# Third mixer with two heads in one product of scores, bias as a product with ones, sink as a column, and other places for the activations' tiles

## The chip, the cores and the metric

One NeuronCore of a Trainium2 chip runs the whole network in one launch. The metric is device time in microseconds (us). Matrix products run on TensorE (PE), elementwise work on VectorE (DVE), ScalarE (ACT) and GpSimd (POOL); transfers are issued from SyncE (SP).

## What is computed

Four layers on 256 tokens of width 1024, in fp32. Each is a half feed-forward block, a mixer and another half feed-forward block, with norms before and after. Layers 0 and 3 have the dilated mixer, layer 1 the differential one, layer 2 the sliding-window mixer with bias and sinks:

```python
for i in range(4):
    x = x + 0.5 * rms_norm(swiglu(rms_norm(x, ...), gate, up, down), ...)
    x = x + rms_norm(mixer_i(rms_norm(x, ...)), ...)
    x = x + 0.5 * rms_norm(swiglu(rms_norm(x, ...), gate, up, down), ...)

def swa_sink_attention(h, w_in, b_in, w_out, sinks):      # layer 2
    proj = h @ w_in + b_in        # 16 query heads of 64, 2 key heads, 2 value heads
    s = q @ k.T / 8 - slope * dist              # masked to the last 128 tokens
    m = max(max(s), sink)
    p = exp(s - m); denom = sum(p) + exp(sink - m)
    return ((p / denom) @ v) @ w_out
```

## The kernel before

A product in fp32 is three products on parts (`mm3`): each operand is split into a high part `h` (a cast to fp32r) and the remainder `l`, and `hi*h`, `hi*l`, `lo*h` are added up in PSUM. Weights stream from HBM into `raw` (three buffers) and are split into `hi` (ScalarE, line 142) and `lo` (VectorE, or GpSimd in the mixers, line 143), four buffers each. Activations are split the same way into `xTh`, `xTl` (normed input, transposed), `hTh`, `hTl` (feed-forward hidden) and `oTh`, `oTl` (a mixer's output).

In `mm3` the first operand is stationary (loaded into the array) and the second moves through it. In a row of the profile, `out<-moving,stationary`. In the feed-forward block, `gu` are the products of 512 columns for gate and up (stationary `xT`, moving weights), `acc` those for the way down (stationary `hT`). In a mixer, `lead` and `v` have `xT` stationary and weights moving, `qk` has weights stationary and `xT` moving; `sc` are scores, `tp` transposes, `o` weighted values; `acc` on `oT` closes the mixer.

A partition of SBUF is filled pool by pool: constants, then `raw`, `hi`, `lo` of 8192 bytes each, then `x`, gains, work tiles and `xTh`, `xTl`, then small tiles, then the block's own tiles, which begin with `hTh`, `hTl` or `oTh`, `oTl`.

The third mixer (`kind == 2`) works in 16 units, one head each, over both blocks of 128 queries. `biased` adds the bias on VectorE while the projection is read from PSUM. `stack_q` and `stack_k` place high and low parts in the two halves of the partitions, so that a head's score takes two products of 128 partitions (line 525) per block of queries. Then come minimum (line 756), exponential (759), the sink's exponential (762), its addition (784), the reciprocal, the normalisation (791), four transposes (800), the split of `p` (817, 818) and the products with `v`. The loop over `slot` works a unit's steps in different slots, with projections (`rest`) and then the closing product in between. A list scheduler sets the order on each engine; queues run in that order. The bias comes from two small transfers: `cbt` at the program's start, `cbv` (line 438) at this mixer's start.

Of the kernel before, what the change touches and what calls it, by code (L numbers as in the profile page):

```python
# [29 lines left out]
NACT = 0  # L30
# [16 lines left out]
def tile_network(  # L47
# [16 lines left out]
    c_bias_t: bass.AP,  # L64
    c_bias_v: bass.AP,
# [119 lines left out]
    cbt = const.tile([P, 9], F32, name="cbt")  # L185
    sink = const.tile([P, 16], F32, name="sink")
    nsink = const.tile([P, 16], F32, name="nsink")
# [34 lines left out]
    def norm_elem(t, s, parts=1):  # L222
# [9 lines left out]
        hn_of[t] = hn  # L232
# [35 lines left out]
    def norm_tr_(t):  # L268
        hn = hn_of.pop(t)
        if t == 0:  # L270
            new_xT()
# [67 lines left out]
    def ffn(layer, which):  # L339
        s = 3 * layer + 2 * which  # L340
        with ExitStack() as c:
            fp = c.enter_context(tc.tile_pool(name="ffn", bufs=2, reuse_waits="tile"))
            hTh = fp.tile([P, KF, SEQ], F32R, name="hTh", bufs=1)
            hTl = fp.tile([P, KF, SEQ], F32R, name="hTl", bufs=1)
# [75 lines left out]
    def mixer(layer):  # L420
# [3 lines left out]
        with ExitStack() as c:  # L424
            mp = c.enter_context(tc.tile_pool(name="mix", bufs=2, reuse_waits="tile"))
            oTh = mp.tile([P, KD, SEQ], F32R, name="oTh", bufs=1)
            oTl = mp.tile([P, KD, SEQ], F32R, name="oTl", bufs=1)
# [60 lines left out]
            def biased(src, bias, sc):  # L488
                tmp = mp.tile([P, SEQ], F32, tag="cq", name="cq", bufs=2)
                dve.tensor_scalar(out=tmp, in0=src, scalar1=bias, scalar2=sc, op0=ALU.add, op1=ALU.mult)  # L490
                return tmp

# [10 lines left out]
            def stack_q(z, e, src, sc):  # L503

                own, other = halves(e)
                if sc is None:
                    act.copy(out=z[own], in_=src[own])
                    dve.tensor_tensor(out=z[other], in0=src[own], in1=z[own].bitcast(F32), op=ALU.subtract)
                    return
# [67 lines left out]
            def token_major(i, k, k0, o, t, step):  # L577
# [581 lines left out]
```

## Time and profile before

| | us |
|---|---|
| median of 3 runs | 2340.42 (2339.28 to 2341.62) |
| the profiled execution | 2340.16 |
| its span, first to last instruction | 2338.4 |
| first mixer | 201 to 486 of the span |
| third mixer | 1370.7 to 1479.8 of the span |

Times in rows are from the span's start. PE ends are modelled, so spacing is read from the starts of successive products. "Idle before" says how long the engine stood before that group, and the arrow what ended it. A row of windows has the engines in the order PE, PEld (loads of the stationary operand), DVE, ACT, POOL, then the granted TensorE clock, the DMA share and GB/s.

### The profile page before, as it was taken

What the parts mean: (1) busy time and instruction counts of PE and PEld (TensorE: products, weight loads), DVE (VectorE), ACT (ScalarE), POOL (GpSimd) and SP (SyncE); (2) the same over time, 40 slices, a digit from 0 to 9 for tenths busy, and PEclk for the clock granted to TensorE, in tenths of its full rate; (3) what the DMA queues carried; (4) which work ended last, traced back from release to release, by engine and by line L of the source; (5) the groups of instructions that cost most, each with busy time, mean ns of one, the idle gap of its engine ahead of it and who ended that gap; (6) DMA issues with size and microseconds to landing.
All of it is one profiled execution on the core that took longest, in us unless ns stands there. A gap on an engine that the chain in (4) does not pass through costs nothing.

```text
span 2338.4 us, 32427 instructions
## 1 busy us (share of the span) xinstructions
PE 2295.4 (98%) x12906; PEld 2012.5 (86%) x12906; DVE 1267.0 (54%) x1858; ACT 1201.3 (51%) x2117; POOL 628.3 (27%) x618
## 2 busy tenths in 40 slices
PE   8999999999999999999999988999999999999998
PEld 6889999988888889788888877788888899998887
DVE  6555444565565555665465459654555544446553
ACT  5445655654444447654354447544444466665442
POOL 0005877620020028610020042100200287774000
PEclk9999999999999999999999999999999999999999
DMA  7544444445555554265455541455454444443552
GB/s 285 195 177 171 163 149 150 153 182 196 181 191 190 187 179 158 77 239 188 180 198 191 188 153 67 180 180 182 186 208 181 181 174 146 143 154 136 216 180 90
DMA packets 60776, 404.71 MB, mean 173 GB/s; under 512 B 7120, under 2 KB 8144, under 8 KB 16592
## 3 DMA queue, kind: packets, MB, share of 16 engines
q1 hardware_dynamic: 60480, 402.57, 47.7%
q8 instruction: 101, 1.65, 0.3%
q14 instruction: 51, 0.42, 0.1%
q10 hardware_dynamic: 144, 0.07, 0.0%
HBM read 401.56 MB, written 1.05 MB: 172 GB/s over the span
## 4 chain that ended last, share of the span: by engine, by line
PE 90%; DVE 4%; ACT 2%; POOL 2%; DMA 1%; issue 1%; SPq 0%; POOLq 0%; DVEq 0%; ACTq 0%
PE gu L177 11%; PE gu L176 11%; PE gu L175 11%; PE acc L175 8%; PE acc L176 8%; PE acc L177 8%; PE qk L175 4%; PE qk L177 4%; PE qk L176 4%; PE v L175 2%; PE v L177 2%; PE v L176 2%; PE tp L369 2%; PE tp L800 1%; PE u L177 1%; PE u L176 1%
## 5 line engine op out<-in xcount | busy, mean ns | idle before, releaser
L142 ACT CAST hi<-raw 128x1024 fp32r<-128x1024 f32 (+2 forms) x970 | 774.6, 844 | 769.2 <-PE gu L177 322.1
L143 DVE TENSOR_TENSOR lo<-raw,hi 128x1024 fp32r<-128x1024 f32 (+1 forms) x546 | 659.5, 1246 | 553.3 <-ACT hi L142 553.3
L143 POOL TENSOR_TENSOR lo<-raw,hi 128x512 fp32r<-128x512 f32 (+1 forms) x424 | 545.5, 1318 | 204.9 <-ACT hi L142 198.2
L175 PE MATMUL gu<-hi,xTh 128*128 128x512 f32 (+1 forms) x1280 | 474.2, 370 | 0.0
L177 PE MATMUL gu<-hi,xTl 128*128 128x512 f32 (+1 forms) x1280 | 471.2, 368 | 0.0
L176 PE MATMUL gu<-lo,xTh 128*128 128x512 f32 (+1 forms) x1280 | 470.9, 368 | 0.0
L215 POOL TENSOR_SCALAR ms<-ssf 128x1 f32<-128x1 f32 x24 | 8.3, 347 | 1415.5 <-ACT junk L244 1414.4
L176 PE MATMUL acc<-lo,hTh 128*128 128x512 f32 x704 | 279.0, 396 | 0.0
L175 PE MATMUL acc<-hi,hTh 128*128 128x512 f32 x704 | 277.1, 394 | 0.0
L177 PEld LDWEIGHTS gu<-hi,xTl 128*128 128x128 f32 x1280 | 241.3, 188 | 39.8
L177 PE MATMUL acc<-hi,hTl 128*128 128x512 f32 x704 | 275.5, 391 | 0.0
L176 PEld LDWEIGHTS gu<-lo,xTh 128*128 128x128 f32 x1280 | 241.4, 189 | 39.3
L175 PEld LDWEIGHTS gu<-hi,xTh 128*128 128x128 f32 x1280 | 241.4, 189 | 39.1
L175 PE MATMUL qk<-xTh,hi 128*128 128x256 f32 x800 | 228.7, 286 | 0.0
L177 PE MATMUL qk<-xTh,lo 128*128 128x256 f32 x800 | 226.0, 282 | 0.0
L176 PE MATMUL qk<-xTl,hi 128*128 128x256 f32 x800 | 225.8, 282 | 0.0
L177 PEld LDWEIGHTS acc<-hi,hTl 128*128 128x128 f32 x704 | 132.2, 188 | 29.9
L175 PEld LDWEIGHTS acc<-hi,hTh 128*128 128x128 f32 x704 | 132.3, 188 | 29.2
L176 PEld LDWEIGHTS acc<-lo,hTh 128*128 128x128 f32 x704 | 132.4, 188 | 26.9
L176 PEld LDWEIGHTS qk<-xTl,hi 128*128 128x128 f32 x800 | 152.6, 191 | 0.1
L177 PEld LDWEIGHTS qk<-xTh,lo 128*128 128x128 f32 x800 | 152.6, 191 | 0.0
L175 PEld LDWEIGHTS qk<-xTh,hi 128*128 128x128 f32 x800 | 152.5, 191 | 0.0
(242 smaller groups left out, 3376.4 us busy)
## 6 DMA issues: line engine op xcount, KB each, us to landing
raw<-in_w_ffn_dram SPq DMA_DIRECT2D x263, 1024.0 KB, 4.8
raw<-in_w_a_qk_dram SPq DMA_DIRECT2D x48, 1024.0 KB, 4.8
raw<-in_w_a_v_dram SPq DMA_DIRECT2D x32, 768.0 KB, 4.3
raw<-in_w_a_out_dram SPq DMA_DIRECT2D x8, 1024.0 KB, 4.8
raw<-in_w_b_qk_dram SPq DMA_DIRECT2D x8, 1024.0 KB, 4.8
gain<-in_g_pre_dram SPq DMA_DIRECT2D x12, 512.0 KB, 6.3
gain<-in_g_post_dram SPq DMA_DIRECT2D x12, 512.0 KB, 8.3
raw<-in_w_b_v_dram SPq DMA_DIRECT2D x4, 1024.0 KB, 4.9
```

Source lines behind the costliest of these rows:

```text
L142: act.copy(out=hi[:, cs], in_=r[:, cs])
L143: eng.tensor_tensor(out=lo[:, cs], in0=r[:, cs], in1=hi[:, cs].bitcast(F32), op=ALU.subtract)
L175: pe.matmul(o, lhsT=a[0], rhs=b[0], start=first, stop=False)
L176: pe.matmul(o, lhsT=a[0], rhs=b[1], start=False, stop=False)
L177: pe.matmul(o, lhsT=a[1], rhs=b[0], start=False, stop=last)
L215: pool.tensor_scalar(out=ms, in0=a, scalar1=b, scalar2=EPS, op0=ALU.add, op1=ALU.add)
L369: pe.transpose(tp[:, i * P:(i + 1) * P], h[:, i * P:(i + 1) * P], ident)
L800: pe.transpose(tp[:, c0:c0 + P], sp[:, i * P:(i + 1) * P], ident)
```

## The change

The third mixer is written anew, and tiles of activations move.

- A unit is now two heads and one block of queries. Keys lie in `kc` (`kch`, `kcl`): the first key head in the first 64 partitions and 256 columns, the second in the others, zeros elsewhere. One `mm3` of 512 columns gives both heads' scores. `stack_q`, `stack_k` and `biased` go from this mixer; `q` is split whole (`store_scaled`).
- The bias comes as a row `cb`: its high part in partition 0, its low part in partition 32, zeros elsewhere. One more product with a tile of ones adds it in PSUM. `cb` is built at the mixer's start from five transfers, each cast by ScalarE and subtracted by VectorE.
- The negated sink is a 257th column of a score's row, written by GpSimd, so the exponential's sum has it.
- `xTh`, `xTl` become one tile `xT`, whose two parts begin 192 bytes later in a mixer; `hT` and `oT` become one tile each. `nsink` gets 64 bytes more, so that weights stay where they were. In the built program the first byte of each tile in a partition, divided by 256, leaves: weights 224 before and after; `xT` 224, after 224 in a feed-forward block and 160 in a mixer; `hT` and `oT` 160, after 224. In the first mixer `pw` leaves 224 and `vh` 160, before and after.

```diff
+    NX, NH = KD * SEQ, KF * SEQ
+    def two(z, o, n):
+        return [z[:, o + i * n:o + (i + 1) * n].rearrange("p (k n) -> p k n", n=SEQ) for i in range(2)]
-    def new_xT():
-        xT["h"] = actp.tile([P, KD, SEQ], F32R, tag="xTh", name="xTh")
-        xT["l"] = actp.tile([P, KD, SEQ], F32R, tag="xTl", name="xTl")
+    def new_xT(s):
+        z = actp.tile([P, 2 * NX + 64], F32R, tag="xT", name="xT")
+        xT["h"], xT["l"] = two(z, 48 if s % 3 == 1 else 0, NX)
...
+            hTh, hTl = two(fp.tile([P, 2 * NH], F32R, name="hT", bufs=1), 0, NH)
...
+            oTh, oTl = two(mp.tile([P, 2 * NX + 48], F32R, name="oT", bufs=1), 0, NX)
...
-                cbv = mp.tile([P, P], F32, name="cbv", bufs=1)
-                nc.sync.dma_start(out=cbv, in_=c_bias_v.partition_broadcast(P))
+                cb = mp.tile([P, D + 256], F32R, name="cb", bufs=1)
+                ones = mp.tile([P, SEQ], F32R, name="ones", bufs=1)
+                pool.memset(cb.bitcast(F32), 0.0)
+                pool.memset(ones.bitcast(F32), 1.0)
+                for i in (4, 0, 1, 2, 3):
+                    cs = slice(i * 256, (i + 1) * 256)
+                    cbf = mp.tile([P, 2, 260], F32, tag="sp", name="cbf", bufs=5)[:, 0, :256]
+                    nc.sync.dma_start(out=cbf[:1], in_=c_bias[:, cs])
+                    act.copy(out=cb[:1, cs], in_=cbf[:1])
+                    dve.tensor_tensor(out=cb[32:33, cs], in0=cbf[:1], in1=cb[:1, cs].bitcast(F32), op=ALU.subtract)
...
-                        tmp = biased(ov[:, f], cbt[:, b:b + 1], qsc[:, 16 + b:17 + b])
-                        qk[gr].append([stack(f"q{f}{e}", 4) for e in range(2)])
-                        for e in range(2):
-                            stack_q(qk[gr][f][e], e, tmp, None)
+                        h, l = pair(f"q{f}", [P, SEQ], 4)
+                        store_scaled(h, l, ov[:, f], qsc[:, 16 + b:17 + b])
+                        qk[gr].append((h, l))
...
+                    if last and bias is not None:
+                        pe.matmul(o, lhsT=ones[:, :P], rhs=bias, start=False, stop=True)
...
-                    tmp = biased(tp[:, :SEQ], cbt[:, 8:9], 1.0)
-                    qk["k"] = [stack(f"k{e}", 1, True) for e in range(2)]
-                    for e in range(2):
-                        stack_k(qk["k"][e], e, tmp)
+                    for i in range(2):
+                        rows = slice(64 * i, 64 * i + 64)
+                        store(kc[0][rows, i], kc[1][rows, i], tp[rows, :SEQ])
...
+                            pe.matmul(of, lhsT=cb[:, b * P:(b + 1) * P], rhs=ones, start=True, stop=False)
...
-                        scores_of(dst, q2[:, bs], k2)
+                    pool.tensor_scalar(out=sp[:, :, 256], in0=nsink.rearrange("p (e i) -> p i e", e=2)[:, hd],
+                                       scalar1=1.0, scalar2=None, op0=ALU.mult)
+                    mm3(sc, (h[:, bs], l[:, bs]), [z.rearrange("p e n -> p (e n)") for z in kc], True, True)
...
-                    act.activation(out=se, in_=nm, func=AF.Exp, bias=sink[:, hd:hd + 1], scale=1.0)
...
-                    dve.tensor_tensor(out=den, in0=den, in1=se, op=ALU.add)
```

Outside the third mixer the order on every engine stays as it was. On VectorE, ahead of that mixer's first scores, before (`vl` the values' low part, `cq` a biased projection, `k`, `q` the stacked halves; line 756 the first minimum):

```order
L481 TENSOR_TENSOR vl<-cvt,vh 128x128
L490 TENSOR_SCALAR cq<-tp,cbt 128x256
L519 TENSOR_TENSOR k_12422<-cq,k_12422 64x256
L519 TENSOR_TENSOR k_12423<-cq,k_12423 64x256
L520 COPY k_12422<-k_12422 64x512
L520 COPY k_12423<-k_12423 64x512
L490 TENSOR_SCALAR cq<-tp,cbt,qsc 128x256 x2
```

and at the same place after:

```order
L448 TENSOR_TENSOR cb<-cbf,cb 1x256 x4
L497 TENSOR_TENSOR vl<-lead,vh 128x128
L497 TENSOR_TENSOR kcl<-tp,kch 64x256 x2
L501 SCALAR_TENSOR_TENSOR q0l<-tp,qsc,q0h 128x256
L771 ISA sp,nm<-sc,dist,nsink 128x256
```

Five instructions for the keys, four on `cq` and four on `q` (the last six of them not shown) that stood before the first minimum have become two on `kcl` and one on `q0l`; those on `cb` are new. On ScalarE at the mixer's start, before (`vh`, `tok` are read from the projections, `xTh` is the second token half):

```order
L226 ACTIVATE hn,ssx<-x 128x1024
L480 CAST vh<-cvt 128x128
L615 COPY tok<-lead 128x128
L617 COPY tok<-lead 128x256 x2
L279 CAST xTh<-tp 128x4x128 x2
```

and after:

```order
L229 ACTIVATE hn,ssx<-x 128x1024
L447 CAST cb<-cbf 1x256
L496 CAST vh<-lead 128x128
L282 CAST xT<-tp 128x4x128
L624 COPY tok<-lead 128x128
L282 CAST xT<-tp 128x4x128
L447 CAST cb<-cbf 1x256 x4
```

The cast of the bias's first piece now stands where `vh` stood; `vh` waits for a bias product on TensorE, which needs that piece.

## Rows read from the trace of the kernel before

**Rows 1.** The page's first part: busy us, share of the span, instructions.

```profile
PE 2295.4 (98%) x12906; PEld 2012.5 (86%) x12906; DVE 1267.0 (54%) x1858; ACT 1201.3 (51%) x2117; POOL 628.3 (27%) x618
```

**Rows 2.** Windows of the first mixer: stretch, length, busy us and instructions by engine.

```profile
201.00:486.00 285.00, 284.57 (x2136) 279.28 (x2135) 144.43 (x312) 178.17 (x400) 200.45 (x184) 1.00 0.44 156
```

**Rows 3.** PE by time: first and last start of four unbroken runs of products.

```profile
42.50 0.40 PE L176 MATMUL gu<-lo,xTh 128*128 128x512 f32 x1
...
63.81 0.40 PE L177 MATMUL gu<-hi,xTl 128*128 128x512 f32 x1
...
145.13 0.39 PE L176 MATMUL acc<-lo,hTh 128*128 128x512 f32 x1
...
196.40 0.40 PE L175 MATMUL acc<-hi,hTh 128*128 128x512 f32 x1
...
231.14 0.28 PE L175 MATMUL qk<-xTh,hi 128*128 128x256 f32 x1
...
238.21 0.28 PE L177 MATMUL qk<-xTh,lo 128*128 128x256 f32 x1
...
261.37 0.28 PE L175 MATMUL o<-pw,vh 128*128 128x256 f32 x1
...
262.61 0.28 PE L177 MATMUL o<-pw,vl 128*128 128x256 f32 x1
```

**Rows 4.** Windows of the third mixer's middle.

```profile
1396.80:1421.90 25.10, 16.08 (x113) 14.63 (x111) 24.30 (x59) 17.93 (x50) 14.26 (x11) 0.92 0.31 119
1421.90:1440.10 18.20, 14.86 (x71) 11.29 (x71) 16.66 (x53) 14.22 (x42) 5.12 (x4) 0.92 0.26 81
1440.10:1462.90 22.80, 21.93 (x110) 17.93 (x110) 20.30 (x72) 17.00 (x52) 2.78 (x3) 0.93 0.07 29
```

**Rows 5.** Waits in that stretch: us in total, times, longest.

```profile
PE tp L800 <- DVE sp L791: 5.6, 6, 3.1
...
PE sc L525 <- DVE q L508: 4.0, 1, 4.0
```

**Rows 6.** Products of line 175: shape, count, busy us and mean ns, idle before.

```profile
L175 PE MATMUL acc<-hi,hTh 128*128 128x512 f32 x704 | 277.1, 394 | 0.0
...
L175 PE MATMUL qk<-xTh,hi 128*128 128x256 f32 x800 | 228.7, 286 | 0.0
...
L175 PE MATMUL v<-hi,xTh 128*128 128x384 f32 x224 | 77.6, 346 | 0.0
...
L175 PE MATMUL lead<-hi,xTh 128*128 128x256 f32 x192 | 55.4, 289 | 1.6 <-ACT xTh L279 0.9 <-DVE u L250 0.7
...
L175 PE MATMUL acc<-hi,oTh 128*128 128x512 f32 x128 | 54.0, 422 | 0.9 <-ACT oTh L881 0.7
...
L175 PE MATMUL v<-hi,xTh 128*128 128x256 f32 x48 | 13.8, 288 | 0.0
```

**Rows 7.** VectorE in that stretch; then one form each of VectorE and GpSimd elsewhere.

```profile
L508 DVE TENSOR_TENSOR q<-cq,q 64x256 fp32r<-64x256 f32 x16 | 9.9, 620 | 0.5
...
L784 DVE TENSOR_TENSOR den<-den,se 128x2 f32<-128x2 f32 x16 | 4.0, 251 | 0.0
L490 DVE TENSOR_SCALAR cq<-tp,cbt,qsc 128x256 f32<-128x256 f32 x6 | 3.0, 540 | 0.3 <-PE tp L627 0.2
...
L485 DVE SCALAR_TENSOR_TENSOR ql<-tp,qsc,qh 128x256 fp32r<-128x256 f32 x3 | 1.5, 485 | 6.8 <-ACT qh L484 6.7
...
L452 POOL MEMSET dg10h<- 64x256 f32 x2 | 0.6, 308 | 0.1
```

**Rows 8.** The third mixer's start by time; last, transfers with KB and us to landing.

```profile
1383.60 0.29 DVE L613 TENSOR_TENSOR cvt<-lead,cbv 128x128 f32<-128x128 f32 x1 [2.96 <-DMA cbv<-in_c_bias_v_dram]
...
1385.48 0.39 PE L175 MATMUL lead<-hi,xTh 128*128 128x256 f32 x1 [0.92 <-ACT xTh L279]
...
1379.00 0.43 SPq L193 DMA_DIRECT2D gain<-in_g_post_dram  x1
...
gain<-in_g_post_dram SPq DMA_DIRECT2D x1, 512.0 KB, 9.3
```

More of the change, by code (lines that the diff above doesn't have):

```diff
@@ L29 @@
 PIECES = 2
-NACT = 0
 RAW = 3
@@ L436, in mixer @@
             elif kind == 2:
-                cbv = mp.tile([P, P], F32, name="cbv", bufs=1)
-                nc.sync.dma_start(out=cbv, in_=c_bias_v.partition_broadcast(P))
+                cb = mp.tile([P, D + 256], F32R, name="cb", bufs=1)
[7 more added lines that the diff above has]
+                    act.copy(out=cb[:1, cs], in_=cbf[:1])
+                    dve.tensor_tensor(out=cb[32:33, cs], in0=cbf[:1], in1=cb[:1, cs].bitcast(F32),
+                                      op=ALU.subtract)
+                kc = [mp.tile([P, 2, SEQ], F32R, name=f"kc{c_}", bufs=1) for c_ in "hl"]
+                for v in kc:
+                    pool.memset(v[:64, 1].bitcast(F32), 0.0)
+                    pool.memset(v[64:, 0].bitcast(F32), 0.0)
             qk = {}
@@ L599, in head @@
                 k = KD // nv if what == "v" else KD
-                yield from token_major(ids[n], k, k * m if what == "v" else 0, o, t, step)
+                c0 = D if what == "kv" else 256 * gr
+                yield from token_major(ids[n], k, k * m if what == "v" else 0, o, t, step,
+                                       cb[:, c0:c0 + 256] if kind == 2 else None)
                 if t:
@@ L607, in head @@
                 if t == 0:
-                    tok[n] = mp.tile([P, 2, 256], F32, tag="sp", name="tok", bufs=(3, 6, 5)[kind])
+                    tok[n] = mp.tile([P, 2, 260 if kind == 2 else 256], F32, tag="sp", name="tok", bufs=(3, 6, 5)[kind])[:, :, :256]
                 if what == "kv":
@@ L611, in head @@
                         vv["v"] = pair("v", [P, 2, P], 1)
-                    vt = mp.tile([P, P], F32, tag="cvt", name="cvt")
-                    dve.tensor_tensor(out=vt, in0=o[:, P:], in1=cbv, op=ALU.add)
-                    store(vv["v"][0][:, t], vv["v"][1][:, t], vt)
+                    store(vv["v"][0][:, t], vv["v"][1][:, t], o[:, P:])
                     act.copy(out=tok[n][:, t, :P], in_=o[:, :P])
@@ L758, in scores @@
-                for _, dst, _, m, dn in parts:
-                    act.activation(out=dst, in_=dst, func=AF.Exp, scale=-1.0, bias=m, accum_out=dn)
-                if kind == 2:
-                    se = small.tile([P, 2], F32, tag="se", name="se")
-                    act.activation(out=se, in_=nm, func=AF.Exp, bias=sink[:, hd:hd + 1], scale=1.0)
-                    st[u] = (spb.rearrange("p b n -> p (b n)"), dnb, se)
+                    b = e
+                    h, l = qk[gr][f]
+                    sp = mp.tile([P, 2, 260], F32, tag="sp", name="sp", bufs=5)
@@ new lines, in scores @@
+                    parts = [(sc[:, i * 256:(i + 1) * 256], sp[:, i], dist[:, b], nm[:, i:i + 1],
+                              den[:, i:i + 1], sl_n[hd + 8 * i], nsink[:, hd + 8 * i:hd + 8 * i + 1], 257)
+                             for i in range(2)]
+                    st[u] = (sp, den, None)
+                for src, dst, d, m, _, sl, init, n in parts:
+                    dve.tensor_tensor_reduce(out=dst[:, :src.shape[-1]], in0=src, in1=d, scale=-sl, scalar=init,
+                                             op0=ALU.add, op1=ALU.min, accum_out=m)
@@ L765, in normalised @@
+                for _, dst, _, m, dn, _, _, n in parts:
+                    act.activation(out=dst[:, :n], in_=dst[:, :n], func=AF.Exp, scale=-1.0, bias=m, accum_out=dn)
             def normalised(u):
-                sp, den, se = st.pop(u)
+                sp, den, _ = st.pop(u)
                 rd = small.tile([P, 2], F32, tag="rd", name="rd")
@@ L783, in normalised @@
                 else:
-                    dve.tensor_tensor(out=den, in0=den, in1=se, op=ALU.add)
                     dve.reciprocal(out=rd, in_=den)
-                    for b in range(2):
-                        v = sp[:, b * 256:(b + 1) * 256]
-                        if b < NACT:
-                            act.activation(out=v, in_=v, func=AF.Copy, scale=rd[:, b:b + 1])
-                        else:
-                            dve.tensor_scalar(out=v, in0=v, scalar1=rd[:, b:b + 1], scalar2=None, op0=ALU.mult)
+                    for i in range(2):
+                        v = sp[:, i, :256]
+                        dve.tensor_scalar(out=v, in0=v, scalar1=rd[:, i:i + 1], scalar2=None, op0=ALU.mult)
                 st[u] = sp
```

76 lines of the change are left out of this document (29 added, 47 removed).

## The prediction

> **What bounds the kernel now.** I read the page's first part, then the engines by stage, then groups of matmuls with their counts, then starting times in the order of time. TensorE is busy for 2295.4 of 2338.4 us [rows 1], and in the first mixer for 284.57 of 285.00 us while VectorE has 144.43, ScalarE 178.17 and GpSimd 200.45 [rows 2]. So there the time is the number of products times the spacing of their starts, and no transfer or other engine is near its limit. Recorded durations do not give that spacing (ends are modelled); the starts do. In an unbroken run of 95 `gu` products of 512 columns they stand 94 steps in 63.81 - 42.50 = 21.31 us apart, 226.7 ns each; 225 `acc` products, also 512 wide, take (196.40 - 145.13)/224 = 228.9 ns; 60 `qk` products of 256 columns (238.21 - 231.14)/59 = 119.8 ns; 12 `o` products of 256 columns only (262.61 - 261.37)/11 = 112.7 ns, or 113 within the rows' rounding [rows 3]. The same shapes, two spacings: what differs is where both operands lie.
>
> The third mixer is another matter. [...] TensorE waits there 4.0 us for the halves `q` and 5.6 us for the normalised `sp`, both of VectorE [rows 5]. VectorE sets the pace of this stretch.
>
> **Part 1: where tiles lie.** In the built program a partition holds the weights `hi`, `lo` at bytes that leave 224 when divided by 256. Before, `xTh` and `xTl` leave 224 too, and `hTh`, `hTl`, `oTh`, `oTl` leave 160. The fast `o` of the first mixer has its moving tile `pw` at 224 and its stationary `vh` at 160: the moving operand 64 bytes higher than the stationary one, modulo 256. `qk` and `gu` have distance 0; `acc` has the same 64 as `o`. So by [rows 3] distance 64 is good at 256 columns (113 against 119.8) and slightly bad at 512 (228.9 against 226.7). After the change `hT` and `oT` leave 224 (distance 0 for `acc`), `xT` in a feed-forward block stays at distance 0, and in a mixer `xT` leaves 160: distance 64 for `lead` and `v`, whose moving operand is the weights, and the mirror image, the moving operand 64 bytes lower, for `qk`, whose moving operand is `xT`. Counts from [rows 6]; each product is three lines, so three times the row's count:
> - `acc` on `hT`: 3 x 704 = 2112 at 228.9 - 226.7 = 2.2 ns: -4.6 us. On `oT` 3 x 128 = 384: -0.8 us. Bounds: 0 if the cause is another, and twice that.
> - `lead` and `v` of 256 columns: 3 x (192 + 48) = 720. The row says 6.8 ns; since runs are cut every few products by a unit's scores and transposes, I take 5: -3.6 us (bounds -4.9 and 0).
> - `v` of 384 columns: 3 x 224 = 672. No row shows this width at distance 64; between -6.8 ns (as at 256) and +2.2 (as at 512) I take -2.3: -1.5 us (bounds -4.6 and +1.5).
> - `qk`: 3 x 800 = 2400, at the mirrored distance, which no run of products in the trace has. The nearest row is `o`: off by a quarter too, same width. With 5 ns: -12.0 us. Bounds: -6.8 ns (-16.3 us) and, if the mirror is on the bad side as distance 64 is at 512 columns, +2.2 ns (+5.3 us).
> Sum: -22.5 us. TensorE has no cover in these stages, so it goes to the end; the other engines of the first mixer have 30% and more left [rows 2].
>
> **Part 2: the third mixer.** Removed from VectorE in the stretch: 16 `q` halves of 620 ns (9.9 us), 8 `cq` of about 540 (4.3), 16 additions of the sink's sum (4.0), together 18.2 us; added: 8 `ql` of 485 ns (3.9) [rows 7]. VectorE goes from 61.3 to 47.0 us. The biased `k` with its four copies, before 1396.8, goes as well; its successor reads PSUM directly. ScalarE loses 16 small exponentials and 16 half casts, and gains 8 scalings; it was not the bound. TensorE: per unit three products of 512 columns in the place of four of 256, 48 x 0.229 - 64 x 0.120 = +3.3 us, and ten bias products of 256 columns, 1.2 us, about half in this stretch. At full clock its own work was 52.9 x 0.92 = 48.7 us; with 3.9 more it is 52.6. VectorE then lies under TensorE, so TensorE becomes the bound of the stretch: 66.1 - 53 = -13.1 us. Bounds: 0 if the chain through scores, minimum, exponential and normalisation still sets the slot, and -16 if the faster spacing shows here too. The sixteen sink columns are GpSimd's; they write two elements a row, so I take them for no longer than a memset of 256 elements, 0.31 us [rows 7], and GpSimd has 14.26 + 5.12 + 2.78 = 22.2 us of work in 66.1 [rows 4]. But four of them stand behind two to four weight pieces each, and an exponential waits for its column. Those pieces ran early in this stretch before also, so I cost it at 0 (bound +3).
>
> The start of that mixer gets worse. Before, VectorE and ScalarE stood behind the bias: `cvt` starts at 1383.60 after 2.96 us of waiting for `cbv`, while TensorE goes on with other heads until 1385.48, where it waits 0.92 us for `xT` [rows 8]. After, TensorE itself stands before the first `lead<-cb,ones`, some 74 products after the mixer's first (1370.7 + 74 x 0.12 = 1379.6). The first piece of the bias has the same place in the queue and goes to one partition in place of 128; I take 1382.5 for it, and 1383.5 with a cast, a subtraction and the wait. So TensorE stands about 4 us, has ten products and eight transposes left, and reaches the second token half at 1386 to 1387, 0.5 to 1.5 us later than before. The clearing of `cb` on GpSimd stands ahead of the second half's root: 1280 columns at 0.31 us for 256 are 1.5 us, hidden by that same wait; bare it would cost those 1.5. The other four pieces are issued behind a weight tile; a gain issued there at 1379.00 lands 9.3 us later [rows 8], at 1388.3, where the next bias products stand at about 1388: 0 to 2 us. With half the bias products I take +2.5 us (bounds 0 and +5). Third mixer: -10.6 us.
>
> **The sum** is made against the profiled execution, 2340.16 us (2338.4 plus 1.8 around the span), 0.3 below the median 2340.42: 2340.2 - 22.5 - 10.6 = 2307.1.
>
> **Rivals.**
> (a) Placement does nothing: the two spacings come from what runs beside, not from the bytes. Against it: `acc` and `gu` are unbroken for dozens of us at different values with the same shape. Then only the third mixer counts: 2340.2 - 10.6 = 2329.6. [...]
> (b) The third mixer gives nothing: VectorE's relief is paid back by the wait for the bias and a chain that stays as long. For it: a unit passes TensorE, VectorE, ScalarE, VectorE and TensorE in a row; against it: the waits of [rows 5] are on work that goes. 2340.2 - 22.5 = 2317.7.
> (c) The mirrored distance is neutral or a little bad for `qk`: in place of -12.0 between 0 and +5.3: 2319 to 2324.
> (d) Slower: the mirrored distance is clearly bad. [...] All else gains 21.1 us; with 2400 products it decides from 8.8 ns each, that is from a spacing of 128.6. At 131 ns the time is 2346. No row shows more than 3 ns of loss by place, so it is unlikely.
>
> **How the numbers follow.** Forecast (both parts, about 2300 to 2314) 0.60; (a) 0.13; (b) 0.09; (c) 0.13; (d) 0.05. The likeliest time is 2307. The range 2296 to 2331 takes in the forecast with the better bounds of `qk` and the third mixer, and (a), (b), (c); it leaves out (d), a part of (a) with a poor third mixer, and more than all better bounds. 0.2% is 4.7 us, about what a measurement of this kernel tells from no change. Slower takes (d) and the tail of (a) in which the bias wait costs more than VectorE's relief: 0.06; the same: 0.05; faster: 0.89.
>
> **What would show it.** Runs of `qk` with starts near 114 ns apart (119.8: a or c; over 125: d); runs of `acc` at 226.7; `lead` near 114; `gu` unchanged at 226.7. In the third mixer VectorE under TensorE between the first scores and the last, a granted clock over 0.95, no wait for `q` halves, and one wait of about 3 us at the first `cb` product. The stage should last about 98 us in place of 109.1. I am wrong if the first mixer keeps its 285 us, or if the third keeps its 109.

## The result: 2317.8 us, two thirds of the forecast gain

The changed kernel takes 2317.82 us (median of 4 runs, 2316.75 to 2318.21); the kernel before took 2339.85 us (2337.72 to 2341.62) on the same chip. The ratio is 0.9906, 95% interval 0.9888 to 0.9923: 22.0 us faster, where 33.1 were forecast (2307). The time lies in the range of 2296 to 2331 and the sign is right; it lies outside the 2300 to 2314 of the forecast's own outcome, and by the number alone it is rival (b), 2317.7, which the experiments rule out. A third of the gain is missing, and the rest of this document says where.

The engines on the changed kernel's page, answering [rows 1]:

```profile
PE 2278.5 (98%) x12900; PEld 1999.8 (86%) x12900; DVE 1251.0 (54%) x1826; ACT 1198.3 (52%) x2098; POOL 633.2 (27%) x640
```

The window of its first mixer, answering [rows 2] (length, then busy us of PE, PEld, DVE, ACT, POOL, then granted clock, DMA share, GB/s):

```profile
200.50:482.30 281.80, 281.34 (x2138) 275.92 (x2137) 144.55 (x312) 178.61 (x400) 200.87 (x184) 1.00 0.44 158
```

The first mixer lasts 281.8 us against 285.0 and is as full of TensorE as before: its products stand closer. By stage, from the first product of each (us; the spans are 2338.4 and 2315.0):

| stage | before | after | difference |
|---|---|---|---|
| the way down of a feed-forward block, 8 of them, each (the last ends with the program: 68.05, 67.35) | 61.81 | 61.33 | -0.48 (all: -3.9) |
| first and last mixer, each | 285.25 | 281.82 | -3.43 (both: -6.9) |
| middle mixer | 131.83 | 132.34 | +0.5 |
| third mixer | 109.11 | 99.19 | -9.9 |
| gate and up behind the third mixer | 129.10 | 125.64 | -3.5 |
| gate and up elsewhere | 125.9 to 127.7 | 125.9 to 127.9 | 0 to +0.2 |

The starts that answer [rows 3], of unbroken runs of the changed kernel: `acc` 225 products (224 steps) from the first to the last row shown, two runs of `qk` of 60 and 47 products, and the twelve `o` of the unit of [rows 3].

```profile
145.26 0.39 PE L174 MATMUL acc<-lo,hT 128*128 128x512 f32 x1
...
196.07 0.39 PE L173 MATMUL acc<-hi,hT 128*128 128x512 f32 x1
...
230.48 0.28 PE L173 MATMUL qk<-xT,hi 128*128 128x256 f32 x1
...
237.43 0.28 PE L175 MATMUL qk<-xT,lo 128*128 128x256 f32 x1
...
270.53 0.28 PE L174 MATMUL qk<-xT,hi 128*128 128x256 f32 x1
...
275.75 0.28 PE L175 MATMUL qk<-xT,lo 128*128 128x256 f32 x1
...
260.45 0.28 PE L173 MATMUL o<-pw,vh 128*128 128x256 f32 x1
...
261.75 0.28 PE L175 MATMUL o<-pw,vl 128*128 128x256 f32 x1
```

`acc` is at (196.07 - 145.26)/224 = 226.8 ns, as forecast. `qk` has **two** values at the same place: 6.95/59 = 117.8 in one run, 5.22/46 = 113.5 in another. And `o`, whose operands keep their distance modulo 256, went from 113 to 1.30/11 = 118. Over all unbroken products of a kind: `qk` 119.5 to 115.5, `lead` of 256 columns 119.6 to 117.7, `v` of 256 119.8 to 114.8, `v` of 384 174.2 to 173.6; `o` 114.8 to 118.0 and the scores `sc` of the dilated mixers 117.1 to 118.9. The last two were in no term of the forecast.

Windows of the third mixer after, answering [rows 4]: the stretch that corresponds to 1396.8 to 1462.9 (same distance to the mixer's end), and its fullest part:

```profile
1394.20:1448.00 53.80, 50.96 (x281) 41.11 (x280) 46.88 (x146) 39.91 (x114) 20.22 (x28) 1.00 0.23 84
1400.00:1440.00 40.00, 37.68 (x212) 30.62 (x211) 38.79 (x123) 32.37 (x94) 14.42 (x22) 1.00 0.23 83
```

TensorE's longest waits in that stretch, answering [rows 5] (us in total, times, longest):

```profile
PE tp L808 <- DVE pw L830: 1.6, 2, 0.8
PE tp L808 <- DVE sp L798: 0.6, 2, 0.4
```

And the mixer's first bias product by time, answering [rows 8]:

```profile
1377.65 0.35 PE L590 MATMUL lead<-cb,ones 128*128 128x256 f32 x1 [1.65 <-DVE cb L448]
```

66.1 us became 53.8 (53 were forecast), the clock is 1.00, the wait for `q` halves is gone. Over the whole stretch VectorE has fallen under TensorE about as written (46.88 and 50.96 us; 47.0 and 52.6 were forecast). But between 1400 and 1440 VectorE is busy for 38.79 of 40 us and TensorE for 37.68: there it has not.

### The profile page after: what moved, and what is told of

Its sections match the earlier page's. It is cut to its first block, busy times and chain, and to the rows that moved or that the text cites. A ratio compares the mean times of both kernels' runs of the same rounds, so it can differ in the third digit from the quotient of the medians.

```text
span 2315.0 us, 32434 instructions
## 1 busy us (share of the span) xinstructions
PE 2278.5 (98%) x12900; PEld 1999.8 (86%) x12900; DVE 1251.0 (54%) x1826; ACT 1198.3 (52%) x2098; POOL 633.2 (27%) x640
## 3 DMA queue, kind: packets, MB, share of 16 engines
q8 instruction: 101, 1.65, 0.3%
## 4 chain that ended last, share of the span: by engine, by line
PE 91%; DVE 3%; POOL 3%; ACT 1%; issue 1%; DMA 1%; SPq 0%; POOLq 0%; DVEq 0%; ACTq 0%
PE gu L174 11%; PE gu L175 11%; PE gu L173 11%; PE acc L175 8%; PE acc L173 8%; PE acc L174 8%; PE qk L173 4%; PE qk L174 4%; PE qk L175 4%; POOL lo L141 2%; PE v L173 2%; PE v L174 2%; PE v L175 2%; PE tp L371 2%; PE tp L808 2%; PE u L173 1%
## 5 line engine op out<-in xcount | busy, mean ns | idle before, releaser
L173 PE MATMUL gu<-hi,xT 128*128 128x512 f32 (+1 forms) x1280 | 474.2, 370 | 0.0
L175 PE MATMUL gu<-hi,xT 128*128 128x512 f32 (+1 forms) x1280 | 471.0, 368 | 0.0
L174 PE MATMUL gu<-lo,xT 128*128 128x512 f32 (+1 forms) x1280 | 470.9, 368 | 0.0
L175 PE MATMUL acc<-hi,hT 128*128 128x512 f32 x704 | 276.1, 392 | 0.0
L174 PE MATMUL acc<-lo,hT 128*128 128x512 f32 x704 | 275.9, 392 | 0.0
L175 PEld LDWEIGHTS gu<-hi,xT 128*128 128x128 f32 x1280 | 241.3, 189 | 39.9
L173 PE MATMUL acc<-hi,hT 128*128 128x512 f32 x704 | 275.6, 391 | 0.0
L174 PEld LDWEIGHTS gu<-lo,xT 128*128 128x128 f32 x1280 | 241.5, 189 | 39.1
L173 PEld LDWEIGHTS gu<-hi,xT 128*128 128x128 f32 x1280 | 241.4, 189 | 39.2
L173 PE MATMUL qk<-xT,hi 128*128 128x256 f32 x800 | 225.7, 282 | 0.0
L174 PE MATMUL qk<-xT,hi 128*128 128x256 f32 x800 | 222.8, 278 | 0.0
L175 PE MATMUL qk<-xT,lo 128*128 128x256 f32 x800 | 222.8, 278 | 0.0
L175 PEld LDWEIGHTS acc<-hi,hT 128*128 128x128 f32 x704 | 132.2, 188 | 28.2
L173 PEld LDWEIGHTS acc<-hi,hT 128*128 128x128 f32 x704 | 132.3, 188 | 26.1
L173 PEld LDWEIGHTS qk<-xT,hi 128*128 128x128 f32 x800 | 151.3, 189 | 0.2
L174 PEld LDWEIGHTS qk<-xT,hi 128*128 128x128 f32 x800 | 150.3, 188 | 0.2
```

What stands on the lines that cost most here:

```text
L173: pe.matmul(o, lhsT=a[0], rhs=b[0], start=first, stop=False)
L174: pe.matmul(o, lhsT=a[0], rhs=b[1], start=False, stop=False)
L175: pe.matmul(o, lhsT=a[1], rhs=b[0], start=False, stop=last)
```

## Experiments

**The two parts apart.** One kernel has only the new places (third mixer as before), the other only the new third mixer, with these three edits against the changed kernel:

```diff
-        z = actp.tile([P, 2 * NX + 64], F32R, tag="xT", name="xT")
-        xT["h"], xT["l"] = two(z, 48 if s % 3 == 1 else 0, NX)
+        z = actp.tile([P, 2 * NX + 48], F32R, tag="xT", name="xT")
+        xT["h"], xT["l"] = two(z, 0, NX)
...
-            oTh, oTl = two(mp.tile([P, 2 * NX + 48], F32R, name="oT", bufs=1), 0, NX)
+            oTh, oTl = two(mp.tile([P, 2 * NX], F32R, name="oT", bufs=1), 0, NX)
```

> The kernel before with only the new places of xT, hT and oT (third mixer as before; the sink's sum of exponentials is put into the den tile so that the small tiles take as much room as after the change). My theory, read from the spacings after: acc stages -3.9 us, the two dilated mixers -3.4 each, middle mixer 0 to +0.5, the old third mixer 0 to -1: the ratio to before 0.9945 to 0.9960, 2327 to 2330 us. The prediction's sum said -22.5 us, 2317.7. Rival (a), place does nothing: 1.000.

> The changed kernel with the places of xT, hT and oT as before; the order of every engine is that of the changed kernel. My theory: third mixer about 99 to 100 us against 109.1, the feed-forward block behind it -3.5 us since TensorE comes to it at full clock, nothing else: -12.5 to -13.5 us, ratio 0.9943 to 0.9947. The prediction's step said -10.6 us. If the FFN's 3.5 us go with the places and not with the mixer: -9.5. Rival (b), third mixer worth nothing: 1.000. With the run of the places alone the two should add up to the change, 0.9906.

Measured: places alone 2329.07 us, ratio 0.9950 (0.9937 to 0.9962); third mixer alone 2328.05 us, 0.9950 (0.9937 to 0.9962); before, on that chip, 2340.66. So -11.6 and -12.6 us, in sum 24.2 against the change's 22.0, within the width of the intervals. Rivals (a) and (b) both fall. Stages with the places alone: way down 61.33, dilated mixers 281.8, middle mixer 132.55, third mixer 108.03; with the mixer alone: 61.80, 285.2, 131.83, 100.09.

The block behind the third mixer gets shorter in both. Its first 10 us in the kernel before, with the places alone, with the mixer alone, and in the changed kernel:

```profile
1479.84:1490.00 10.16, 10.04 (x30) 7.64 (x31) 6.29 (x7) 3.46 (x5) 1.69 (x2) 0.68 0.77 248
```

```profile
1474.33:1484.40 10.07, 9.95 (x39) 7.70 (x39) 6.29 (x7) 3.62 (x5) 1.69 (x2) 0.87 0.73 231
```

```profile
1471.39:1481.40 10.01, 10.01 (x48) 8.32 (x47) 7.06 (x7) 5.60 (x8) 2.49 (x4) 1.00 0.75 267
```

```profile
1464.94:1475.00 10.06, 10.06 (x48) 8.37 (x47) 7.16 (x8) 5.62 (x8) 2.52 (x4) 1.00 0.80 294
```

Only part of this is a gain. TensorE waits 3.6 us before and 4.4 us after for `hn`, the next block's normed input, and works at a lower granted clock behind that wait (0.50 and 0.69). The wait and what follows it, first before, then after:

```profile
PE tp L276 <- DVE hn L230: 3.6, 1, 3.6
1479.84:1486.00 6.16, 6.04 (x13) 4.31 (x14) 5.41 (x7) 2.87 (x4) 1.69 (x2) 0.50 0.78 241
```

```profile
PE tp L279 <- DVE hn L233: 4.4, 1, 4.4
1459.46:1464.94 5.48, 5.48 (x21) 4.25 (x22) 4.57 (x6) 3.75 (x6) 0.00 (x0) 0.69 0.71 262
```

Before, eight transposes followed the wait, and the block then ran its first 6.2 us at 0.50. After, 13 of the mixer's closing products stand among those transposes, so the low clock falls on them (0.69 for 5.5 us), in time counted to the third mixer, and the block begins at full clock (1.00 in its first 10.1 us). (So the order does change at this seam, though "The change" says that it stays outside the third mixer.) The two stages have to be read together: 238.2 us before, 224.8 after, -13.4. In the kernels below, which all have the new third mixer, 5.2 to 6.8 us pass from the end of that wait to the block, so the third mixer's length alone is uncertain by 1.5 us.

**The spacing by itself.** The network is left out; only products run, at distances of the two operands in steps of 32 bytes, and no other engine.

> The disputed cost alone: the network is left out (the output is not the reference's). Two pairs of tiles, weights W and activations X, high and low parts 8192 bytes apart as in the kernel, and nothing else running; X starts 0, 32, 64, ... bytes further on. At each distance 144 products of the form of qk (W stationary, X moving, 256 columns) and of lead (X stationary, W moving, 256 columns) for 0 to 992 bytes; 72 of 512 and 96 of 384 columns (X stationary) for 0 to 480. My theory, that the spacing depends on the distance of the two operands alone: qk about 119.7 ns at 0 and 115.5 at 192; the lead form about 119.7 at 0 and 115 to 118 at 192; 512 columns 226.8 at 0 and about 229 at 192. If the period were 256 bytes, as the prediction took it, each curve repeats after 256 bytes and 256 is as slow as 0; the loss of o after the change speaks for 512 or more, then 256 differs from 0. Rival, that the two spacings come from the other engines' traffic and not from the place: all curves are flat within 0.5 ns.

Mean ns from start to start, by how far X begins behind W:

```text
bytes   qk form 256   lead form 256   512 cols   384 cols
  0       120.0          120.0          226.7      173.6
 32       117.8          118.3          233.3      173.3
 64       117.8          117.8          233.4      174.7
 96       119.9          117.3          234.2      176.7
128       118.7          118.6          232.4      176.0
160       117.3          120.0          233.4      176.7
192       113.4          117.8          229.0      173.3
224       118.3          117.8          233.3      176.6
256 and on: the same again, within 0.1
```

First and last start of 144 products of the qk form at 0, then at 192, then of the lead form at 192 (`b<-moving,stationary`):

```profile
25.62 0.28 PE L99 MATMUL b<-X,W 128*128 128x256 f32 x1
...
42.77 0.28 PE L101 MATMUL b<-X,W 128*128 128x256 f32 x1
...
128.08 0.28 PE L99 MATMUL b<-X,W 128*128 128x256 f32 x1
...
144.29 0.28 PE L101 MATMUL b<-X,W 128*128 128x256 f32 x1
...
682.35 0.28 PE L99 MATMUL b<-W,X 128*128 128x256 f32 x1
...
699.20 0.28 PE L101 MATMUL b<-W,X 128*128 128x256 f32 x1
```

17.15, 16.21 and 16.85 us over 143 steps: 119.9, 113.4, 117.8. With no other engine at work the spacing still follows the places, and the period is 256 bytes, as the prediction had it. In this run, where each distance is entered from the one 32 bytes below, 192 is the one good place for `qk`, and at 512 columns every place but 0 costs. The table answers the traces: `acc` before (192) 229.0 against 228.9, `gu` (0) 226.7. But the lead form gets 117.8, not 113, at the distance of the fast `o` of [rows 3].

**Is it a longer period?** The mixer tiles had moved by 256 bytes, so modulo 512 `vh` and `pw` had changed their distance. One line puts it back:

```diff
-            oTh, oTl = two(mp.tile([P, 2 * NX + 48], F32R, name="oT", bufs=1), 0, NX)
+            oTh, oTl = two(mp.tile([P, 2 * NX + 112], F32R, name="oT", bufs=1), 0, NX)
```

> The changed kernel with every tile of a mixer behind oT 256 bytes further on, order of every engine the same. vh is then again 64 bytes below pw modulo 512, as before the change (after it: 64 modulo 256, but 192 below modulo 512... that is 320 apart). If the period is 512: o of the first mixer from 118.0 back to about 114.8 ns, 768 products of the two dilated mixers -2.4 us; sc with it if it is the same cause. If the period is 256, as the prediction took it: o stays at 118.0 and nothing moves.

Measured 2318.57 us, and `o` at 117.95 ns over 380 products: unchanged. That idea falls, in agreement with the table.

**What ran just before.** The two values of `qk` after the change sort by neighbour. Leaving out each run's first eight products, 30 of the 36 runs behind transposes go at 113.3, and all 42 runs behind scores at 117.7 to 118.0. The trace before has both values too, for `o` at one and the same place: 24 runs of twelve behind `qk` go at 113.4, as in [rows 3], and the eight behind scores or `acc` at 117.8 or more. One of those behind scores, (455.48 - 454.18)/11 = 118.2 ns:

```profile
454.18 0.28 PE L175 MATMUL o<-pw,vh 128*128 128x256 f32 x1
...
455.48 0.28 PE L177 MATMUL o<-pw,vl 128*128 128x256 f32 x1
```

So runs were entered from different work, again with nothing beside TensorE.

> The network is left out (the output is not the reference's). Runs of 48 products at the mixers' places (W leaves 224, X 160 modulo 256): the form of qk (moving 192 ahead of the stationary) and of lead (64 ahead), each entered from different work: 512 columns at distance 0, four transposes, 384 columns, 12 or 24 products at distance 0, the own form, or six score-like products with both operands 0, 32, ... 224 bytes apart; once each after a run of 512 columns, after a wait for ScalarE, and after transposes; then six turns of 48 qk and six scores. Nothing else runs. Theory L, formed from the changed kernel's trace (qk runs go at 113.5 after a run of qk and at 118 after scores; o goes at 113.5 before the change and at 118 after it at an unchanged distance modulo 256 and 512): at this distance there are two steady spacings, 113.4 and 117.8, and what runs just before selects one, which then holds for the whole run: so here, too, both appear, qk after scores at distance 0 at 117.8. Rival, that the slower value is other engines' traffic in the kernel: every qk run here is at 113.4 and every lead run at 117.8, whatever ran before. Open, with no forecast: at which distance of the scores qk is left at 113.4.

Spacing of 48 products, slow first steps left out, by what ran before; in each cell the three beginnings (512 columns, a wait, transposes):

```text
entered from                       qk form, 192        lead form, 192
nothing more                       117.7 113.6 117.8   117.8 123.5 117.7
384 columns                        117.8 117.8 117.8   117.8 117.8 117.8
24 of the qk form at distance 0    113.3 113.3 113.3   113.3 113.3 113.3
12 of the lead form at distance 0  113.3 113.3 113.3   113.3 113.3 113.3
6 scores at distance 0             117.8 113.3 117.8   117.8 117.8 117.8
six turns of qk and scores:
  scores at 0                      117.8 every time
  scores at 64                     113.3 two times of the last five
  scores at 160                    113.3 three times of the last five
```

In the run of 123.5 the first half of the products goes at 127.7 and the second at 117.7. Not in the table: with scores at 32, 96, 128, 192 and 224, one, none, none, none and two of the last five turns were fast; and a run of the own form before `qk` left it at 117.7, 113.3 and 117.8 by the three beginnings. So what stands right before does not always decide alone. First and last start of the qk form behind 24 products at distance 0, then behind six scores:

```profile
81.00 0.29 PE L114 MATMUL b<-X,W 128*128 128x256 f32 x1
...
86.35 0.28 PE L116 MATMUL b<-X,W 128*128 128x256 f32 x1
...
162.24 0.28 PE L114 MATMUL b<-X,W 128*128 128x256 f32 x1
...
167.77 0.28 PE L116 MATMUL b<-X,W 128*128 128x256 f32 x1
```

5.35 and 5.53 us over 47 steps. At these two distances there are two steady spacings, 113.3 and 117.8, and the work before selects one, which then holds for the run. This also fits `o`: before the change its 24 runs stood behind `qk` at distance 0, the entry that gives 113.3 every time; after it, behind `qk` at 117.8, all 24 go at 118.1. Whether other distances have a second spacing was not run, and why an entry selects one or the other is not shown.

**The same in the kernel.** Both kernels have the bias built early (below) and move tiles of the scores; no engine's order changes. The second against the kernel with the bias early:

```diff
+                    if gr == 0:
+                        mp.tile([P, 16], F32, name="gap0", bufs=1)
                     k2 = [stack(f"k{e}", 2, True) for e in range(2)]
...
+                    if gr == 0 and e == 0:
+                        mp.tile([P, 32], F32, name="gap1", bufs=1)
                     h, l = pair("qg", [P, SEQ], 4)
```

> The changed kernel with the bias built early, and in the dilated mixers the tiles qg 96 bytes further on: the three products of a score's second part then have moving and stationary operand 160 bytes apart modulo 256 in place of 0; every engine's order is the same. In the bare run the runs of qk after such scores went at 117.8 and 113.3 in turn (after scores at distance 0: always 117.8). Theory L: about half of the qk products of the dilated mixers that now go at 118 (about 1000 of 2400 by the trace after) go at 113.5: -1 to -2.5 us over both mixers, each 281.8 to 280.5 to 281.3; o follows in the runs that stand behind them. Rival, that in the kernel the slower value is held by other engines' traffic: 281.8 as before, spacing 115.4.

> As the run before, but with k2 64 bytes further on and qg 192: all five products of a score are 64 bytes apart. In the bare run two of five runs of qk after such scores went at 113.3. Theory L: a gain of the same kind and a little less, 0 to -2 us over both mixers; and if both distances give the same spacing as distance 0 does, L's entry rule does not carry over from the bare run to the kernel.

Measured: dilated mixers 280.33 and 280.36 us in place of 281.8, both -1.45 each; `qk` 114.8 and 114.9 ns, `o` back at 114.8 and 114.9. Medians 2314.98 and 2312.41 us, ratios 0.9887 (0.9870 to 0.9903) and 0.9882 (0.9867 to 0.9896). The twelve `o` with the scores 64 apart, (261.60 - 260.35)/11 = 113.6 ns:

```profile
260.35 0.28 PE L173 MATMUL o<-pw,vh 128*128 128x256 f32 x1
...
261.60 0.28 PE L175 MATMUL o<-pw,vl 128*128 128x256 f32 x1
```

And 60 `qk` behind scores 64 apart, (237.71 - 231.01)/59 = 113.6 ns, where the changed kernel's first `qk` run above has 117.8:

```profile
231.01 0.28 PE L173 MATMUL qk<-xT,hi 128*128 128x256 f32 x1
...
237.71 0.28 PE L175 MATMUL qk<-xT,lo 128*128 128x256 f32 x1
```

In both kernels all 42 runs of `qk` behind scores settle at 113.3, and the 24 runs of `o` behind `qk` are back at 113.5. The entry rule carries over, the rival of other engines' traffic falls. The gain of 2.9 us over both mixers is more than was expected (at most 2.5 and 2), since in the bare run only some runs behind such scores were fast.

**The start of the third mixer.** The bias row is built in the feed-forward block before:

```diff
+                    bp = c.enter_context(tc.tile_pool(name="bias", bufs=1))
+                    at_use(state["use"] + 6, lambda: make_bias(bp))
...
-                cb = mp.tile([P, D + 256], F32R, name="cb", bufs=1)
-                ones = mp.tile([P, SEQ], F32R, name="ones", bufs=1)
...
+                cb, ones = bias["cb"], bias["ones"]
```

> The changed kernel with the bias row and the tile of ones built during layer 2's first feed-forward block instead of at the third mixer's start (same arithmetic, same places of weights, xT, oT, q, k, v). The prediction's step 'the start of that mixer gets worse, +2.5 us': the trace after has TensorE waiting 1.65 us at the first bias product. If that wait was the whole cost, third mixer 99.2 to 97.5 us and the total -1.7 us (2316 from 2317.8). If the clearing of cb on GpSimd and the casts ahead of the norm's second half cost as well: -2 to -3. If the wait only covers something that comes late anyway (the second half of xT): 0 to -0.5.

Measured: the stage 96.76 us in place of 99.19, -2.4, of which 2.2 are there at the first scores; the total 2315.29 us (2315.05 to 2316.66). So the start did cost about what the prediction charged (+2.5), although the wait at the first bias product alone is 1.65. Part of that comes back elsewhere: the gate and up before the mixer takes 127.6 us in place of 126.6, and the profiled spans differ by 1.3 us.

**Which engine bounds the middle of the third mixer.** First, half of VectorE's normalisation is left out:

> The changed kernel with the bias built early and without half of VectorE's normalisation in the third mixer: the division of the second head's scores is left out (16 operations of about 523 ns, 8.4 us of VectorE). The prediction's step was that VectorE, relieved by the change, falls under TensorE and TensorE becomes the bound of the stretch; then the stage stays at 96.8 us, to -0.5. The trace after has VectorE busy for 9.5 to 9.9 of every 10 us between 1400 and 1440 and TensorE for 8.6 to 10.0; if VectorE still sets the pace there, the stage falls by what TensorE stands in it, 2 to 2.5 us, to 94.5.

The stage falls from 96.76 to 95.04 us. From 1400 to 1440 VectorE goes from 38.51 to 34.50 and TensorE from 37.76 to 38.20:

```profile
1400.00:1440.00 40.00, 37.76 (x208) 30.42 (x207) 38.51 (x123) 31.00 (x89) 13.05 (x21) 1.00 0.22 80
1400.00:1440.00 40.00, 38.20 (x215) 31.66 (x214) 34.50 (x109) 30.94 (x92) 13.58 (x21) 1.00 0.23 80
```

So VectorE still cost up to 1.7 us, less than expected; one profile against one decides little here, as the next comparison shows. More telling was the run with the scores 64 apart: there the same third mixer took 100.15 us, 3.4 more than with the bias early, at the same order of instructions. One operation on VectorE did it, by time:

```profile
1394.76 3.59 DVE L792 TENSOR_SCALAR sp<-sp,rd 128x256 f32<-128x256 f32 x1
```

Beside it GpSimd split three weight pieces:

```profile
1394.49 3.72 POOL L141 TENSOR_TENSOR lo<-raw,hi 128x512 fp32r<-128x512 f32 x3
```

The instructions of that line (count, then minimum, median and maximum in ns):

```profile
L792 DVE TENSOR_SCALAR sp<-sp,rd x32: 331/344/3593, 1393.8 to 1440.0; 128x256 f32<-128x256 f32 x32
```

And TensorE's wait for them:

```profile
PE tp L802 <- DVE sp L792: 3.3, 2, 2.9
```

In the changed kernel the eight normalisations that overlap GpSimd's splitting take 1.06 us on average, the other 24 take 0.34; minima and subtractions, which read PSUM, take the same beside that splitting and away from it (means of 0.475 and 0.478 us, 0.685 and 0.682). Taking the suspected cause away, GpSimd's low halves of the last five weight tiles:

```diff
-        lo = wp.tile([P, 2048], F32R, tag="lo", name="lo")
+        lo = hi if i in thin else wp.tile([P, 2048], F32R, tag="lo", name="lo")
...
+                if i not in thin:
                     eng.tensor_tensor(out=lo[:, cs], in0=r[:, cs], in1=hi[:, cs].bitcast(F32), op=ALU.subtract)
```

> The kernel of the run with the scores 64 bytes apart, with one part left out: GpSimd's low halves of the last five weight tiles of the third mixer (20 pieces of 1.25 us); the products read the high part in their place, so their number is unchanged. In the profiles VectorE's normalisation (128x256, SBUF to SBUF) takes 0.34 us where GpSimd is idle and 0.9 to 1.3 us, once 3.6, where it splits weights, while minima and subtractions that read PSUM take the same time in both. Theory: these two engines stand in each other's way there. Then all 32 normalisations take 0.34 to 0.35 us, 11 us in all in place of 16 to 18, TensorE's wait for the first normalised scores (2.9 us) is gone, and the stage falls from 100.1 to 95 to 96.7 us. Rival: the length comes from the data or from ScalarE; then single ones stay above 0.8 us.

The normalisation's line in that run (minimum, median, maximum), and below it the window:

```profile
L796 DVE TENSOR_SCALAR sp<-sp,rd x32: 333/346/354, 1394.0 to 1433.6; 128x256 f32<-128x256 f32 x32
```

```profile
1400.00:1440.00 40.00, 39.97 (x216) 32.48 (x216) 33.66 (x116) 30.11 (x87) 1.97 (x9) 1.00 0.15 53
```

All 32 take 0.33 to 0.35 us, TensorE is busy for 39.97 of 40 us, the stage takes 94.38 (95 to 96.7 were expected), the total 2310.02. Up to the wait for `hn` that is 87.9 us, against 94.6 in the kernel that it was made from and 91.5 with the bias early. Without GpSimd in the way TensorE is the bound all along, as the prediction's step has it; with it, not from 1400 to 1440.

**Two versions.** One moves part of the normalisation to ScalarE, one keeps it on VectorE in another form, which writes out the sum of its row. That this form would not be held up beside GpSimd was the author's estimate; no run had shown it. Its edit:

```diff
+                        if u < 10:
+                            dve.tensor_scalar(out=v, in0=v, scalar1=rd[:, i:i + 1], scalar2=0.0, op0=ALU.mult,
+                                              op1=ALU.add, accum_out=den[:, i:i + 1])
+                        else:
                             dve.tensor_scalar(out=v, in0=v, scalar1=rd[:, i:i + 1], scalar2=None, op0=ALU.mult)
```

> A version: the changed kernel with the bias built early, scores of the dilated mixers 64 bytes apart, and the normalisation of the first head in the third mixer's first ten units on ScalarE. If VectorE, held up by GpSimd, still sets the pace up to 1440, the third mixer takes 94.5 to 96.5 us (96.8 and 100.1 in the two profiles before), and the total 2310 to 2312 us, ratio 0.987 to 0.988. If ScalarE (8 to 8.6 of 10 us busy there) becomes the bound: 97 to 99 us and no gain over 2312.

> As the run with the scores 64 bytes apart, but VectorE's normalisation of the third mixer's first ten units (those beside GpSimd's splitting) also writes out the sum of its row, which nobody reads. [...] Rival: it is held up like the plain form: single ones above 1 us, and the stage is longer by the added reads, 97 to 101.

The same two views of the kernel with the sum written out:

```profile
L793 DVE TENSOR_SCALAR_CACHE_REDUCE sp<-sp,rd x20: 468/475/481, 1393.3 to 1419.2; 128x256 f32<-128x256 f32 x20
```

```profile
1400.00:1440.00 40.00, 39.64 (x214) 32.06 (x213) 34.91 (x126) 29.66 (x86) 10.97 (x17) 1.00 0.19 72
```

With ScalarE: stage 95.62 us, 2311.36 us, ratio 0.9877 (0.9861 to 0.9894). With the sum written out: no operation over 481 ns, TensorE waits 0.4 us for normalised scores, stage 95.53 us, 2310.72 us (2309.36 to 2313.25), ratio 0.9879 (0.9862 to 0.9895). At least five of these operations (1393.26 to 1397.3) overlap two stretches of GpSimd's splitting, of 2.58 and 3.82 us, and take 0.47 to 0.48 us; the plain operation took 3.59 us beside a stretch of 3.72. By the medians, which come from different chips, the versions beat the changed kernel by 6.5 and 7.1 us; between the two no run decides. Most of that is the scores' places and the early bias: against the kernel with the scores 64 apart they lie only 1.0 and 1.7 us lower (ratios 0.9877 and 0.9879 against 0.9882), which is within the intervals. The profile of that kernel is of its longest execution (2315.52 us; the other three 2311.99 to 2312.72), so its 100.15 us need not be usual, and the 4.5 us between the stages in the profiles are not the versions' gain.

## Why the prediction was right in sign and a third too high

Its steps one by one, gains in us:

- **The premise, distance modulo 256, decides the spacing.** Right: the bare run has the period to 0.1 ns. What failed is that a distance has one spacing. The prediction read 113 from `o` of [rows 3] as the price of its place; it was the price of its place behind `qk` at distance 0, an entry that the change itself removed. Eight other runs of `o` in the same trace, behind scores or `acc`, had the slow value.
- **`acc`: 4.6 on `hT`.** 3.9 (2112 products, 1.86 ns less). On `oT` 0.2 in place of 0.8. Right, a little small.
- **`qk`: 12.0.** 4.0 ns over 2400 products are 9.7. The value forecast, near 114, exists: the slow entries behind scores make the mean 115.5. Rivals (c) and (d), the mirror image neutral or bad, fall: in the bare run the mirrored place is the best of eight.
- **`lead` and `v` of 256 columns: 3.6.** 1.9 ns over 576 `lead` and 5.0 over 144 `v` are 1.8. `lead` should have been near 114; it stays at its slow value, 117.8.
- **`v` of 384: 1.5.** 0.4 (0.6 ns). The interpolation between 256 and 512 columns was not a row, and was wrong.
- **`o` and `sc` unchanged: 0.** They lost 3.2 ns over 384 and 1.9 over 320 products, 1.8 in all. This was the missing term.
- **TensorE has no cover.** True in the dilated mixers, not in the middle one. There the faster products are worth 2.5 us and the stage got 0.5 longer: TensorE waited for VectorE instead, as its waits in that mixer before and after show. In the kernels above with the same middle mixer it takes 131.3 to 132.6 us, so the faster products' 2.5 us came to between 0.7 us lost and 0.5 us gained there.

```profile
PE o L175 <- DVE osb L863: 1.9, 4, 0.7
PE tp L891 <- DVE oTl L894: 1.3, 1, 1.3
```

```profile
PE o L173 <- DVE osb L875: 3.4, 4, 1.6
PE tp L903 <- DVE oT L906: 2.4, 3, 1.4
```

- **Third mixer: 10.6.** 9.0 alone, 9.9 with the places, whose terms there were 1.4 more; with the block behind it, where the low clock had fallen before, 13.4. The stretch (13.1 forecast, 12.3 measured), the start (2.5 and 2.4), the stage (98 and 99.2), the clock (over 0.95 and 1.00) and the lost wait came as written, and VectorE's load in the stretch too (47.0 and 46.9). The 66.1 us of the stretch before, with 61.3 of VectorE and 52.9 of TensorE, are the sums over the windows of [rows 4]. What the step "VectorE lies under TensorE, so TensorE becomes the bound" missed is that a sum over 66 us hides a part: six of the eight normalisations that GpSimd's splitting holds up lie between 1400 and 1440, and TensorE waits there for VectorE. The price is the 3.6 us between 91.5 and 87.9 us up to the wait for `hn` (bias early, with and without the splitting). The operations were priced at their means [rows 7], and these held GpSimd's interference: in the trace before, four of the 16 `q` halves take 1.2 us beside GpSimd's splitting, the other twelve 0.42, and five normalisations take over 1.2. No term of the prediction says what working beside GpSimd costs VectorE.
- **The block behind it: 0.** It got 3.5 us shorter, in no step; the low clock that it lost (0.50 for 6.2 us) now lies on the third mixer's closing products (0.69 for 5.5 us).

By stage the forecast's terms were 13.4 in the dilated mixers, 3.1 in the middle one, 12.0 in the third with the block behind it and 4.6 in the way down; 6.9, -0.5, 13.4 and 3.9 came. That is 6.5 + 3.6 - 1.4 + 0.7 = 9.4 short; the forecast's 33.1 and the 23.4 by which the spans differ are 9.7 apart. So the missing third lies in the dilated and the middle mixers, in part 1.

## What to carry to other kernels

Where TensorE is full, the offset of two operand tiles modulo 256 bytes was worth up to 6% of a product of 256 columns (113.3 to 120.0 ns); read it from the starts of all runs, and check by what a run is entered, since at one distance 113.3 and 117.8 ns both occurred. The places that made `qk` faster (119.5 to 115.5 ns) changed its neighbours' spacing too (`o` 114.8 to 118.0), so every kind in the stage needs a term. Where VectorE looks full, split the durations of one form into those beside GpSimd's work and those away from it before pricing its removal, and where the two overlap try a form that reads PSUM or writes an accumulator (here 0.46 to 0.49 us for the minima and 0.47 to 0.48 for the normalisation with its sum written out, where the plain one took 0.34 clear and 1.06 beside GpSimd). Where TensorE waits at the seam of two stages, read both together: here the low clock behind the wait lay on the next block before (0.50 for 6.2 us) and on the mixer's closing products after (0.69 for 5.5 us).

## What the runs showed of the hardware that was not expected

- Two stable spacings of identical products at one distance, 113.3 and 117.8 ns, selected by the work before and kept for the run, with every other engine idle.
- At 512 columns distance 0 is best (226.7; elsewhere 229.0 to 234.2 ns), at 256 columns nothing in the table is slower (120.0).
- One VectorE operation of 0.34 us stretched to 3.59 us by three operations of GpSimd; the same operation with its sum written out was not held up in any of 20 (at most 0.481 us), at least five of them beside GpSimd's splitting.
- The third mixer of one order of instructions took 96.8 us in one profile and 100.1 in two others, 3.1 us of it by that one collision.
- Behind TensorE's wait for `hn` (3.6 us before, 4.4 after) the granted clock was low, and the order of the products behind the wait decided which stage paid: 0.50 for the first 6.2 us of the next block before, 0.69 for 5.5 us on the mixer's closing products in the changed kernel. With the places alone that block's first 10.1 us ran at 0.87, with the mixer alone its first 10.0 at 1.00. What sets the length is open.
